# One scan for both directions: the backward state-space chunks fed in reverse, 159 columns instead of 190

## Chip, core and metric

The kernel runs on one core of one Trainium2 chip. The metric is the device time of one execution in microseconds (us). The engines are TensorE (PE; its weight loads are PEld), VectorE (DVE), ScalarE (ACT), GpSimd (POOL) and SyncE (SP), which issues most DMAs. They run in parallel, each in its own order of instructions, and wait for one another by semaphores.

## What is computed

One layer of a diffusion backbone: 1024 latent tokens and 256 context tokens of width 1024. A modulated RMS norm feeds one combined input projection, whose columns go to four head groups (convolution, Fourier mixing, neighbourhood attention, and a bidirectional state space); their outputs are normed, concatenated and projected, and a squared-ReLU MLP follows. The change lies in the state space, cut here to what matters:

```python
for dirn, reverse in ((0, False), (1, True)):
    lam = lax.complex(a_re[dirn], a_im[dirn])               # 16 groups x 64 states
    dt = jnp.exp(log_dt[dirn])[:, None]
    a_bar = jnp.exp(lam * dt)
    b_bar = ((a_bar - 1) / lam)[..., None] * lax.complex(b_re[dirn], b_im[dirn])
    c_mat = lax.complex(c_re[dirn], c_im[dirn])
    h_c = diag_scan(a_bar, jnp.einsum("blgm,gpm->blgp", ucc, b_bar), reverse)
    h0 = h_c[:, 0] if reverse else h_c[:, -1]                # the context's last state
    bu_x = jnp.einsum("blgm,gpm->blgp", uxc, b_bar)
    bu_x = bu_x.at[:, edge].add(a_bar * h0)
    h_x = diag_scan(a_bar, bu_x, reverse)
    y_x = y_x + jnp.einsum("blgp,gmp->blgm", h_x, c_mat).real
```

## The kernel before, in words

The order around the state space is not written by hand: a scheduler orders each engine's instructions by a modelled timeline, and tiles come from pools that are stacked in the on-chip memory; a tile that lies where an earlier one lay waits for that one's readers. So a change of size in one pool can move instructions far from it.

The first 130 us hold the modulation (`gv_rows`, L151), the norm of the latent tokens (`nt`, `xl`), the first projection tiles, and the context's norm and products (L210, L242 to L244). A projection tile is 24 matmuls of 128x512 (L364), three for each of eight chunks, on weights that ScalarE and GpSimd split into a high and a low part (`whi`, `wlo`, L231 to L235).

The state space works on chunks of eight tokens: 16 channels by 8 tokens make the 128 rows of `U` (columns: 32 chunks of context, 128 of latent tokens, and the 32 of context again). Partitions 0 to 63 hold the forward states, 64 to 127 the backward ones.

- *Small setup* (pools `ssm` and `tiny`, L434 to L581): from `log_dt` by exponential, sine and powers (tiles `t_...`, `pw`, `pa`, `pb`) to the input weights `bb`, on GpSimd and VectorE in turn, most of it 16 columns wide.
- *`ssm_setup(b)`*, for each of eight batches of two groups: GpSimd and VectorE make `wn` (the chunk's input weights; TensorE transposes them by `pt` into `wt`) and `ca` (its output weights); ScalarE copies parts of `ca` into the zero-padded `cx_`; TensorE makes the chunk's inner kernel `pk` from it, which goes through DRAM into the Toeplitz tile `tz`.
- *`ssm_tables(b)`*: sine and cosine of the phase of each chunk index (`nidx`), on VectorE and ScalarE.
- *`ssm_main(b)`*: the chunk products `ps` (L682) over NQ = 190 columns; a rotation by the tables (`ro`, L687 to L692, VectorE and GpSimd); the scans with the real decay (L697 forward, L698 backward with its operands read in reverse), 64 partitions each; the rotation back (`hr`, L701 to L706); and the output products `py`, three for each group (L710 `tz` by `U`, L711 and L712 `ca` by `hr`).

Setup and tables of batch b+1 are written ahead of main b. Beside all that TensorE runs projection tiles. The convolution's input `cv` (L782) comes after them, on VectorE, when its tile is done.

Of the kernel before, what the change touches and what calls it, by code (L numbers as in the profile page):

```python
# [8 lines left out]
F32 = mybir.dt.float32  # L9
# [3 lines left out]
ALU = mybir.AluOpType  # L13
# [4 lines left out]
P = 128  # L18
# [4 lines left out]
MAGIC = 12582912.0  # L23
TWO_PI = 6.2831845
PI_ = 3.14159225
NQ = 190

COLS = {}
_n = 0
# [20 lines left out]
def body(tc, A, out, dbg=None):  # L50
    nc = tc.nc
    V, S, G, PE, SP = nc.vector, nc.scalar, nc.gpsimd, nc.tensor, nc.sync
# [349 lines left out]
    for hf in range(2):  # L402
        for ti in FIRST:
            o = x_tile(cw[ti], hf, (("mm", "gn"), ("at", "gv"))[hf][ti == 8])
# [14 lines left out]
    for m in range(2):  # L419
        o = c_tile(cw[12 + m])  # L420
# [15 lines left out]
    sp = open_pool("ssm", "right", stack=sset)  # L436
# [141 lines left out]
    bm = sp.tile([P, 2, 16, 32], F32, name="bm")  # L578
# [4 lines left out]
    GB = 2  # L583
# [9 lines left out]
    def tms(name, w):  # L593
        return sp.tile([P, GB, w], F32, name=name, tag="ss", bufs=4)

    cx_ = sp.tile([P, 2, GB, 240], F32, name="cx_")
    G.memset(cx_, 0.0)

    def ssm_setup(b):
        g0 = GB * b  # L600
        gs = slice(g0, g0 + GB)

        pbx = lambda t: t[:, :, gs].rearrange("p j g -> p g j")[:, :, :, None].to_broadcast([P, GB, 8, 16])
        bbx = lambda t: t[:, gs, None, :].to_broadcast([P, GB, 8, 16])
        wn = [tms(f"wn{i}", P) for i in range(2)]
        t1, t2 = tms("ws1", P), tms("ws2", P)
        G.tensor_tensor(v4(wn[0]), pbx(pb_r), bbx(bb_r), ALU.mult)
        G.tensor_tensor(v4(t1), pbx(pb_i), bbx(bb_i), ALU.mult)
        V.tensor_tensor(wn[0], wn[0], t1, ALU.subtract)
        G.tensor_tensor(v4(wn[1]), pbx(pb_r), bbx(bb_i), ALU.mult)  # L610
        G.tensor_tensor(v4(t2), pbx(pb_i), bbx(bb_r), ALU.mult)
        V.tensor_tensor(wn[1], wn[1], t2, ALU.add)

        ca = sp.tile([P, 2, GB, 160], F32, name="ca", tag="ca", bufs=3)
        pax = lambda t: t[:, :, gs].rearrange("p s g -> p g s")[:, :, :, None].to_broadcast([P, GB, 10, 16])
        cx = lambda i: b3(cn[:, i, :])[:, gs, None, :].to_broadcast([P, GB, 10, 16])
        t1, t2 = tms("cs1", 160), tms("cs2", 160)
        G.tensor_tensor(v4(ca[:, 0]), pax(pa_r), cx(0), ALU.mult)
        G.tensor_tensor(v4(t1), pax(pa_i), cx(1), ALU.mult)
        G.tensor_tensor(ca[:, 0], ca[:, 0], t1, ALU.subtract)  # L620
        G.tensor_tensor(v4(ca[:, 1]), pax(pa_r), cx(1), ALU.mult)
        G.tensor_tensor(v4(t2), pax(pa_i), cx(0), ALU.mult)
        V.scalar_tensor_tensor(ca[:, 1], ca[:, 1], -1.0, t2, ALU.mult, ALU.subtract)

        pk = st_tile("pk")
        fw, bw = slice(0, 64), slice(64, 128)
        S.copy(cx_[fw, :, :, 112:240], ca[fw, :, :, 0:128])
        S.copy(cx_[bw, :, :, 0:128], ca[bw, :, :, 32:160])
        for g in range(GB):
            for i in range(2):  # L630
                PE.matmul(pk[32 * g:32 * g + 32, 0:240], bm[:, i, g0 + g, :], cx_[:, i, g, :],
                          start=i == 0, stop=i == 1, skip_group_check=True)
        kt_ = sp.tile([32 * GB, 240], F32, name="kt_", tag="kt_", bufs=2)
        S.copy(kt_, pk[:32 * GB, :240])
        V.scalar_tensor_tensor(kt_[:, 112:128], K("idk")[:32 * GB], C("ssm_d", b)[:32 * GB],
                               kt_[:, 112:128], ALU.mult, ALU.add)
        tz = sp.tile([P, GB, P], F32, name="tz", tag="tz", bufs=3)
        for g in range(GB):
            o_ = (g0 + g) * 240
            SP.dma_start(ap(kb, o_, [[3840, 16], [1, 240]]), kt_[32 * g:32 * g + 16, :])  # L640
            SP.dma_start(tz[:, g, :], ap(kb, o_, [[16, 8], [3840, 16], [1, 128]]))
        wt = sp.tile([P, GB, 2, P], F32, name="wt", tag="wt", bufs=3)
        pt = st_tile("pt")
        for g in range(GB):
            for i in range(2):
                PE.transpose(pt[:, (2 * g + i) * P:(2 * g + i + 1) * P], wn[i][:, g, :], ident)
        S.copy(wt.rearrange("p a b c -> p (a b c)"), pt[:, :2 * GB * P])
        return ca, tz, wt

    def ssm_tables(b):  # L650

# [16 lines left out]
        V.tensor_scalar(fl(cst_), fl(cst_), -2.0, 1.0, ALU.mult, ALU.add)  # L668
        return snt, cst_

    def ssm_main(b, ca, tz, wt, snt, cst_):
        g0 = GB * b
        U = sp2.tile([P, GB, 192], F32, name="U", tag="U", bufs=2)
        for g in range(GB):
# [2 lines left out]
        Ss = sp2.tile([P, 2, GB, NQ], F32, name="Ss", tag="Ss", bufs=2)  # L677
        for g in range(GB):
            ps = at_tile("ps")
            for i in range(2):  # L680
                for d in range(2):
                    PE.matmul(ps[64 * d:64 * d + 64, i * NQ:(i + 1) * NQ], wt[:, g, i, 64 * d:64 * d + 64],  # L682
                              U[:, g, 2 * d:2 * d + NQ], start=True, stop=True, skip_group_check=True)
            S.copy(Ss[:, :, g, :], ps[:, :2 * NQ].rearrange("p (i q) -> p i q", i=2))
        s_r, s_i = fl(Ss[:, 0]), fl(Ss[:, 1])
        r1, r2, r3, r4 = [tmp(f"ro{i}", NQ, t) for i, t in enumerate(("ra", "rc", "rb", "rc"))]
# [5 lines left out]
        V.tensor_tensor(fl(r3), fl(r3), fl(r4), ALU.subtract)  # L692
        for i, src in ((0, r1), (1, r3)):
            for g in range(GB):
                f_, b_ = slice(0, 64), slice(64, 128)
                r_ = rho[:, g0 + g:g0 + g + 1].to_broadcast([P, NQ])
                V.tensor_tensor_scan(Ss[f_, i, g, :], r_[f_], src[f_, g, :], 0.0, ALU.mult, ALU.add)  # L697
                V.tensor_tensor_scan(Ss[b_, i, g, ::-1], r_[b_], src[b_, g, ::-1], 0.0, ALU.mult, ALU.add)  # L698
        xs = slice(31, 159)
        h1, h2_, h3, h4 = [tmp(f"hr{i}", P, t) for i, t in enumerate(("ra", "rc", "rb", "rc"))]  # L700
        V.tensor_tensor(h1, Ss[:, 0, :, xs], cst_[:, :, xs], ALU.mult)  # L701
# [6 lines left out]
        for g in range(GB):  # L708
            o = py[:, g * P:(g + 1) * P]
            PE.matmul(o, tz[:, g, :], U[:, g, 32:160], start=True, stop=False)  # L710
            PE.matmul(o, ca[:, 0, g, 16:144], h1[:, g, :], start=False, stop=False)  # L711
            PE.matmul(o, ca[:, 1, g, 16:144], h3[:, g, :], start=False, stop=True)  # L712
        yt = tmp("yt", P, "yt")
        S.copy(fl(yt), py[:, :GB * P])
        for g in range(GB):
# [26 lines left out]
    for tb in range(10):  # L742
        o = mm_tile()
        pairs = []
        for k in range(8):
            if tb < 8:
                hf, b = divmod(tb, 4)
                a_, b_ = hh[hf][k][:, b * P:(b + 1) * P], hl[hf][k][:, b * P:(b + 1) * P]
            else:
                b = tb - 8  # L750
                a_, b_ = ch[k][:, b * P:(b + 1) * P], cl[k][:, b * P:(b + 1) * P]
# [91 lines left out]
    for m in range(2):  # L843
        t = q4("eo")
# [22 lines left out]
    for m in range(2):  # L867
# [25 lines left out]
    for m in range(2):  # L893
# [6 lines left out]
        f = q4("ff")  # L900
# [13 lines left out]
    for hf in range(2):  # L914
        sl = slice(hf * H, (hf + 1) * H)
        yf = q4("yf").rearrange("p (m c) -> p m c", m=2)
        for m in range(2):
            ms = slice(m * P, (m + 1) * P)
            o = (at_tile, st_tile)[m]("fo")
# [509 lines left out]
    for k in range(3, 8):  # L1429
# [3 lines left out]
        o = mm_tile()  # L1433
# [444 lines left out]
def shape_constants():  # L1878
# [6 lines left out]
        bd[0, s, s] = np.cos(ang) / 256  # L1885
        bd[1, s, s] = np.sin(ang) / 256
    nidx = np.zeros((P, NQ))
    nidx[:64] = np.arange(NQ)
    nidx[64:] = NQ - 1 - np.arange(NQ)
    sel = np.zeros((P, 2))  # L1890
    for q in range(4):
        for v in range(2):
# [42 lines left out]
```

## Time and profile before

| | us |
|---|---|
| median of 3 runs (1337.73 to 1339.29) | 1338.77 |
| the profiled execution, its own time | 1341.13 |
| its span in the trace | 1339.0 |
| TensorE busy in the span | 1197.4 (89%) |
| VectorE busy | 1068.4 (80%) |
| GpSimd busy | 808.6 (60%) |
| ScalarE busy | 652.7 (49%) |

The profiled execution took 2.13 us more than its span, and 2.36 more than the median. Shares over the whole span mix stages with different limits, so the state space is read by stretches: it lies between 127.7 us (the first `ps`) and 270 us (the last `py`), and the convolution begins at 282.7.

### The profile page before, as it was taken

The numbers are of one execution on the slowest core, as the hardware profiler recorded it, in microseconds if no ns is written. First come the engines' busy times: TensorE is split into PE (matmuls) and PEld (weight loads), VectorE is DVE, ScalarE is ACT, GpSimd is POOL, SyncE is SP. The second block draws the span as 40 slices with busy tenths as digits, with TensorE's granted clock in tenths as the row PEclk, the third lists the DMA queues.
The fourth block names the chain that finished last, engine by engine and source line by source line (L and its number), as shares of the span: only waits on it lengthen the run. The fifth ranks groups of instructions, "written<-read, shape, count | busy, mean of one in ns | idle before, by whom it ended". The sixth has DMA issues, their size and how long they took to land.

```text
span 1339.0 us, 18718 instructions
## 1 busy us (share of the span) xinstructions
PE 1197.4 (89%) x6188; PEld 965.5 (72%) x6188; DVE 1068.4 (80%) x1636; ACT 652.7 (49%) x1337; POOL 808.6 (60%) x1002
## 2 busy tenths in 40 slices
PE   5889878898865999899999999999999999999996
PEld 3657656777655777777778777777877777777775
DVE  4775999869999768658695579888888888888867
ACT  5254333323446565554664445555545555444555
POOL 3825677372556734015367477777877778787754
PEclk9989898998975999898999999999999999999998
DMA  9455232161153544323121121111211112211113
GB/s 344 142 164 164 81 125 79 47 199 66 51 177 94 175 128 142 109 78 143 32 77 43 40 64 32 48 56 56 63 56 32 52 52 63 64 41 39 56 40 126
DMA packets 75058, 121.77 MB, mean 91 GB/s; under 512 B 16977, under 2 KB 35154, under 8 KB 74962
## 3 DMA queue, kind: packets, MB, share of 16 engines
q1 hardware_dynamic: 62802, 113.24, 26.9%
q10 hardware_dynamic: 12160, 7.34, 1.8%
q8 instruction: 49, 0.80, 0.3%
q14 instruction: 47, 0.39, 0.1%
HBM read 106.68 MB, written 13.88 MB: 90 GB/s over the span
## 4 chain that ended last, share of the span: by engine, by line
PE 48%; DVE 29%; ACT 5%; issue 4%; POOL 4%; DMA 3%; SPq 1%; ACTq 0%; DVEq 0%; POOLq 0%
PE fa L1472 11%; PE qa L1472 6%; PE qb L1472 5%; PE fb L1472 5%; DVE cacc L1015 5%; DVE tl L1488 3%; PE fc L1472 2%; DVE fl L1488 2%; PE f L1472 2%; PE p_t L1270 2%; PE mm L1097 2%; PE mm L1472 2%; DVE Ss L698 2%; DVE Ss L697 1%; DVE X L1493 1%
## 5 line engine op out<-in xcount | busy, mean ns | idle before, releaser
L1456 POOL TENSOR_TENSOR w2l<-w2r,w2h 128x128 fp32r<-128x128 f32 (+1 forms) x232 | 177.4, 766 | 75.3 <-ACT w2h L1455 68.1
L1493 DVE SCALAR_TENSOR_TENSOR X<-fa,gt2c,X 128x512 f32<-128x512 f32 x216 | 159.4, 745 | 13.0 <-PE fa L1472 13.0
L1455 ACT ACTIVATE w2h<-w2r 128x128 fp32r<-128x128 f32 (+1 forms) x232 | 85.8, 387 | 150.8 <-POOL w2r L1706 79.8
L1456 POOL TENSOR_TENSOR w2l<-w1r,w2h 128x256 fp32r<-128x256 f32 x136 | 108.5, 814 | 57.7 <-ACT w2h L1455 34.0
L235 POOL TENSOR_TENSOR wlo<-wraw,whi 128x1024 fp32r<-128x1024 f32 x30 | 75.2, 2508 | 102.0 <-ACT whi L233 82.9
L1493 DVE SCALAR_TENSOR_TENSOR X<-fb,gt2c,X 128x512 f32<-128x512 f32 x108 | 80.5, 745 | 35.4 <-PE fb L1472 35.3
L1456 POOL TENSOR_TENSOR w2l<-ws,w2h 128x256 fp32r<-128x256 f32 x84 | 67.9, 815 | 41.4 <-ACT w2h L1455 40.1
L1015 DVE SCALAR_TENSOR_TENSOR cacc<-cv,wdw,cacc 128x512 f32<-128x512 f32 x92 | 92.3, 1047 | 0.6
L364 PE MATMUL mm<-xl,whi 128*128 128x512 f32 x192 | 81.2, 424 | 3.8 <-DVE xl L220 3.8
L364 PE MATMUL mm<-xh,whi 128*128 128x512 f32 x192 | 77.3, 423 | 7.0 <-ACT xh L218 5.8
L1472 PE MATMUL fa<-th,w2h 128*128 128x512 f32 x156 | 63.2, 405 | 19.7 <-DVE X L1493 19.7
L364 PE MATMUL mm<-xh,wlo 128*128 128x512 f32 x192 | 80.6, 420 | 0.0
L1455 ACT ACTIVATE w2h<-w1r 128x256 fp32r<-128x256 f32 x136 | 53.9, 409 | 47.5 <-DVE w1r L1609 16.5
L1472 PE MATMUL qa<-cb,w2h 128*128 128x512 f32 x224 | 70.7, 397 | 0.7 <-ACT ft L1624 0.7
L1488 DVE TENSOR_TENSOR fl<-ft,fh 128x512 fp32r<-128x512 f32 x64 | 56.9, 906 | 12.8 <-ACT fh L1487 12.7
L1472 PE MATMUL fa<-th,w2l 128*128 128x512 f32 x156 | 61.7, 396 | 0.6 <-POOL w2l L1456 0.6
L1472 PE MATMUL fa<-tl,w2h 128*128 128x512 f32 x156 | 61.5, 394 | 0.0
L1013 POOL TENSOR_TENSOR pacc<-pacc,ptmp 128x512 f32<-128x512 f32 x24 | 37.4, 1559 | 29.8 <-ACT ptmp L1012 29.8
L1455 ACT ACTIVATE w2h<-ws 128x256 fp32r<-128x256 f32 x84 | 33.1, 410 | 42.4 <-DVE ws L1605 20.4
L1472 PEld LDWEIGHTS fa<-th,w2h 128*128 128x128 f32 x156 | 29.3, 188 | 30.8 <-DVE X L1493 25.2
L364 PEld LDWEIGHTS mm<-xh,whi 128*128 128x128 f32 x192 | 38.1, 201 | 18.4 <-ACT xh L218 7.2
L1472 PEld LDWEIGHTS qa<-cb,w2h 128*128 128x128 f32 x224 | 42.0, 188 | 11.2 <-ACT ft L1624 1.1
(788 smaller groups left out, 3945.3 us busy)
## 6 DMA issues: line engine op xcount, KB each, us to landing
w2r<-in_w_ff SPq DMA_DIRECT2D x68, 256.0 KB
wmB<-in_wmodB SPq DMA_DIRECT2D x32, 512.0 KB
w1r<-in_w_ff SPq DMA_DIRECT2D x64, 256.0 KB
wm<-in_wmodA SPq DMA_DIRECT2D x16, 512.0 KB
wraw<-in_w_in SPq DMA_DIRECT2D x12, 512.0 KB
x<-in_xT SPq DMA_DIRECT2D x8, 512.0 KB
wraw<-in_w_out SPq DMA_DIRECT2D x8, 512.0 KB
kr<-k_d SPq DMA_DIRECT2D x16, 256.0 KB
```

Source lines behind the costliest of these rows:

```text
L235: (lo_eng or G).tensor_tensor(lo, raw, hi.bitcast(F32), ALU.subtract)
L364: PE.matmul(o, a_[:, k, :], b_[hf][k], start=k == 0 and i == 0, stop=k == 7 and i == 2)
L698: V.tensor_tensor_scan(Ss[b_, i, g, ::-1], r_[b_], src[b_, g, ::-1], 0.0, ALU.mult, ALU.add)
L1013: G.tensor_tensor(pacc, pacc, t, ALU.add)
L1015: V.scalar_tensor_tensor(acc, x(k), w(k), acc, ALU.mult, ALU.add)
L1097: PE.matmul(o, a_[:, 2 * kk + c, :], b_, start=c == 0 and i == 0, stop=c == 1 and i == 2)
L1270: PE.matmul(po[:, j * 64:j * 64 + 64], ptt[:, i * P:(i + 1) * P], rv, start=i == 0, stop=i == 4, skip_group_check=True)
L1455: S.activation(hi, a, AF.Copy)
L1456: G.tensor_tensor(lo, a, hi.bitcast(F32), ALU.subtract)
L1472: PE.matmul(o, a_[:, i, :], m_, start=start and j == 0, stop=stop and j == 2, skip_group_check=True)
L1488: V.tensor_tensor(lo, t, hi.bitcast(F32), ALU.subtract)
L1493: return V.scalar_tensor_tensor(x, o, gt2(k), x, ALU.mult, ALU.add).ins
```

## The change

NQ goes from 190 to 159. The backward half of `ps` reads `U` in reverse, from its last column down, so that both directions run in the same sense: one scan does all 128 partitions (L701 after), 32 scans for 64, and all tables and rotations are 159 columns wide. The chunk index `nidx` counts upward on all partitions. Since the backward states now stand in reverse, one product can't take both directions to the output: `h1` and `h3` have each one product with the forward weights and one with the backward weights that reads `hr` in reverse (L716, L717 after), which makes five for three in each group. These weights are taken from the zero-padded tile, which grows from 240 to 272 columns and has three buffers (`cx0` to `cx2`), each held until its batch's output; `ca` has one buffer instead of three.

```diff
-NQ = 190
+NQ = 159
...
-    cx_ = sp.tile([P, 2, GB, 240], F32, name="cx_")
-    G.memset(cx_, 0.0)
+
+
+    cxs = [sp.tile([P, 2, GB, 272], F32, name=f"cx{i}") for i in range(3)]
+    for t in cxs:
+        G.memset(t, 0.0)
...
-        ca = sp.tile([P, 2, GB, 160], F32, name="ca", tag="ca", bufs=3)
+        ca = sp.tile([P, 2, GB, 160], F32, name="ca", tag="ca", bufs=1)
+        cx_ = cxs[b % 3]
...
-        S.copy(cx_[fw, :, :, 112:240], ca[fw, :, :, 0:128])
-        S.copy(cx_[bw, :, :, 0:128], ca[bw, :, :, 32:160])
+        S.copy(cx_[fw, :, :, 128:272], ca[fw, :, :, 0:144])
+        S.copy(cx_[bw, :, :, 0:144], ca[bw, :, :, 16:160])
...
-                PE.matmul(pk[32 * g:32 * g + 32, 0:240], bm[:, i, g0 + g, :], cx_[:, i, g, :],
+                PE.matmul(pk[32 * g:32 * g + 32, 0:240], bm[:, i, g0 + g, :], cx_[:, i, g, 16:256],
...
-                              U[:, g, 2 * d:2 * d + NQ], start=True, stop=True, skip_group_check=True)
+                              U[:, g, 191:191 - NQ:-1] if d else U[:, g, 0:NQ], start=True, stop=True,
+                              skip_group_check=True)
...
-                f_, b_ = slice(0, 64), slice(64, 128)
                 r_ = rho[:, g0 + g:g0 + g + 1].to_broadcast([P, NQ])
-                V.tensor_tensor_scan(Ss[f_, i, g, :], r_[f_], src[f_, g, :], 0.0, ALU.mult, ALU.add)
-                V.tensor_tensor_scan(Ss[b_, i, g, ::-1], r_[b_], src[b_, g, ::-1], 0.0, ALU.mult, ALU.add)
+                V.tensor_tensor_scan(Ss[:, i, g, :], r_, src[:, g, :], 0.0, ALU.mult, ALU.add)
...
-            PE.matmul(o, ca[:, 0, g, 16:144], h1[:, g, :], start=False, stop=False)
-            PE.matmul(o, ca[:, 1, g, 16:144], h3[:, g, :], start=False, stop=True)
+
+            for i, h in enumerate((h1, h3)):
+                PE.matmul(o, cx_[:, i, g, 144:272], h[:, g, :], start=False, stop=False)
+                PE.matmul(o, cx_[:, i, g, 0:128], h[:, g, ::-1], start=False, stop=i == 1)
...
-    nidx[:64] = np.arange(NQ)
-    nidx[64:] = NQ - 1 - np.arange(NQ)
+    nidx[:] = np.arange(NQ)
```

The pool `ssm` grows by 4096 bytes a partition: `cx_` and three buffers of `ca` were 11,520 bytes, three `cx` and one `ca` are 15,616. The pool `tiny` above it slides by as much, and its first tiles come to lie where the modulation's `gv_rows` lies. The engines' orders differ in many places, of which three matter here.

On VectorE, the chain of small tiles (`t_dr`, L454, is its first step that needs `log_dt`) stood among the modulation's and the norm's operations. Before:

```order
L215 SCALAR_TENSOR_TENSOR nt<-x,gsc,acc 128x512
L210 TENSOR_TENSOR acc<-acc,sq 128x512 x2
L220 SCALAR_TENSOR_TENSOR xl<-nt,mod,xh 128x512
L210 TENSOR_TENSOR acc<-acc,sq 128x512 x5
L454 SCALAR_TENSOR_TENSOR t_dr<-t_dn,t_ldt 128x16
L455 SCALAR_TENSOR_TENSOR t_dr<-t_dn,t_dr 128x16
L458 SCALAR_TENSOR_TENSOR t_dw<-t_dw,t_dr 128x16
```

After, at the end of the modulation:

```order
L215 SCALAR_TENSOR_TENSOR nt<-x,gsc,acc 128x512 x2
L220 SCALAR_TENSOR_TENSOR xl<-nt,mod,xh 128x512 x2
L497 MEMSET pw_r 128x16
L498 MEMSET pw_i 128x16
L509 RECIPROCAL t_iv<-t_iv 128x16
L210 TENSOR_TENSOR acc<-acc,sq 128x256 x7
L454 SCALAR_TENSOR_TENSOR t_dr<-t_dn,t_ldt 128x16
L455 SCALAR_TENSOR_TENSOR t_dr<-t_dn,t_dr 128x16
L458 SCALAR_TENSOR_TENSOR t_dw<-t_dw,t_dr 128x16
```

The chain moved behind the last `xl` and behind the context's sum of squares, the seven `acc` of 128x256; all of the setup follows it.

On GpSimd, the place of the first rotation `ro`, in the main part of batch 0. The numbers in the names tell the batches' tiles apart: `wn_1438` and `cs_1449` are batch 3's, and those of the row `cs_1336` are batch 2's. Before:

```order
L676 COPY U<-U 128x2x32
L608 TENSOR_TENSOR ws_1440<-pb_i,bb_i 128x256
L676 COPY U<-U 128x2x32
L610 TENSOR_TENSOR wn_1439<-pb_r,bb_i 128x256
L688 TENSOR_TENSOR ro_1287<-Ss,snt 128x380
L690 TENSOR_TENSOR ro_1289<-Ss,snt 128x380
L611 TENSOR_TENSOR ws_1441<-pb_i,bb_r 128x256
L619 TENSOR_TENSOR cs_1449<-pa_i,cn 128x320
L622 TENSOR_TENSOR cs_1450<-pa_i,cn 128x320
L702 TENSOR_TENSOR hr_1305<-Ss,snt 128x256
L704 TENSOR_TENSOR hr_1307<-Ss,snt 128x256
L688 TENSOR_TENSOR ro_1400<-Ss,snt 128x380
```

After (line numbers are three to five higher), first the rows from batch 0's last `ca` on, through batch 1's setup (`wn_1216`, `cs_1227`):

```order
L624 TENSOR_TENSOR ca<-ca,cs_1170 128x320
L610 TENSOR_TENSOR wn_1216<-pb_r,bb_r 128x256
L611 TENSOR_TENSOR ws_1218<-pb_i,bb_i 128x256
L622 TENSOR_TENSOR ca<-pa_r,cn 128x320
L613 TENSOR_TENSOR wn_1217<-pb_r,bb_i 128x256
L625 TENSOR_TENSOR ca<-pa_r,cn 128x320
L614 TENSOR_TENSOR ws_1219<-pb_i,bb_r 128x256
L623 TENSOR_TENSOR cs_1227<-pa_i,cn 128x320
L626 TENSOR_TENSOR cs_1228<-pa_i,cn 128x320
L624 TENSOR_TENSOR ca<-ca,cs_1227 128x320
```

and directly behind them, with batch 2's setup (`wn_1329`, `cs_1340`):

```order
L610 TENSOR_TENSOR wn_1329<-pb_r,bb_r 128x256
L611 TENSOR_TENSOR ws_1331<-pb_i,bb_i 128x256
L622 TENSOR_TENSOR ca<-pa_r,cn 128x320
L625 TENSOR_TENSOR ca<-pa_r,cn 128x320
L613 TENSOR_TENSOR wn_1330<-pb_r,bb_i 128x256
L693 TENSOR_TENSOR ro_1291<-Ss,snt 128x318
L695 TENSOR_TENSOR ro_1293<-Ss,snt 128x318
L614 TENSOR_TENSOR ws_1332<-pb_i,bb_r 128x256
L623 TENSOR_TENSOR cs_1340<-pa_i,cn 128x320
L705 TENSOR_TENSOR hr_1305<-Ss,snt 128x256
L707 TENSOR_TENSOR hr_1307<-Ss,snt 128x256
L626 TENSOR_TENSOR cs_1341<-pa_i,cn 128x320
```

Before, three batches' setup was done and a fourth begun when the first `ro` came. After, one batch's setup precedes these rows, fourteen setup products of the next two stand between it and the first `ro`, and there are two setup products, for three, between the pair of `ro` and the pair of `hr`.

On TensorE, the place of the first `ps`, batch 0's, before:

```order
L364 MATMUL mm<-xh,wlo 128x512
L364 MATMUL mm<-xh,whi 128x512
L682 MATMUL ps<-U,wt 64x190 x8
L631 MATMUL pk<-cx__1153,bm 32x240 x4
L646 MATMUL pt<-ident,wn_1325 128x128
L646 MATMUL pt<-ident,wn_1326 128x128
L646 MATMUL pt<-ident,wn_1325 128x128
L646 MATMUL pt<-ident,wn_1326 128x128
L364 MATMUL mm<-xl,whi 128x512
```

And the place of the first `pk` and `pt`, batch 0's too, after:

```order
L364 MATMUL mm<-xh,wlo 128x512
L635 MATMUL pk<-cx_1153,bm 32x240 x4
L650 MATMUL pt<-ident,wn_1159 128x128
L650 MATMUL pt<-ident,wn_1160 128x128
L650 MATMUL pt<-ident,wn_1159 128x128
L650 MATMUL pt<-ident,wn_1160 128x128
L364 MATMUL mm<-xh,whi 128x512
L364 MATMUL mm<-xl,whi 128x512
L364 MATMUL mm<-xh,wlo 128x512
L242 MATMUL mm<-ch,whi 128x256
```

Before, the `pk` and `pt` of two batches had come long before the first `ps`, and 175 projection matmuls of 128x512 and 72 context products stood ahead of it. After, the first `pk` comes 20 context products and three wide ones ahead of the first `ps`, which has 192 and 92 ahead of it. At the other end, 47 matmuls of projection tiles that the convolution needs stand ahead of the last batch's `py` on `hr`, and 24 before.

## Rows read from the trace of the kernel before

**Rows 1.** Stretches of the one core; the header names the columns.

```profile
core 0: us, PE busy (x) PEld busy (x) DVE busy (x) ACT busy (x) POOL busy (x), PEclk, DMA share, GB/s
0.00:28.00 28.00, 13.35 (x71) 9.06 (x75) 13.82 (x38) 15.77 (x27) 6.24 (x15) 1.00 0.96 353
...
54.00:82.00 28.00, 23.93 (x136) 17.52 (x135) 26.20 (x45) 10.00 (x18) 18.44 (x24) 0.94 0.39 131
...
127.70:282.70 155.00, 131.03 (x852) 103.69 (x852) 133.48 (x192) 50.92 (x106) 97.17 (x93) 0.91 0.31 95
129.70:270.10 140.40, 116.55 (x775) 92.00 (x769) 131.04 (x185) 47.12 (x101) 89.29 (x86) 0.90 0.26 79
272.50:282.70 10.20, 10.20 (x46) 8.19 (x45) 0.03 (x2) 2.49 (x3) 5.59 (x7) 1.00 0.73 243
282.70:420.00 137.30, 108.74 (x482) 89.51 (x480) 134.38 (x169) 58.34 (x89) 70.08 (x44) 0.85 0.37 116
```

**Rows 2.** TensorE's timeline: start, us, line, operation, operands, count [idle before].

```profile
127.69 1.51 PE L682 MATMUL ps<-U,wt 128*64 128x190 f32 x16
...
132.19 0.38 PE L710 MATMUL py<-U,tz 128*128 128x128 f32 x2
132.33 0.48 PE L364 MATMUL mm<-xh,wlo 128*128 128x512 f32 x1
...
141.68 0.49 PE L711 MATMUL py<-hr,ca 128*128 128x128 f32 x2 [2.18 <-DVE hr L705]
...
270.22 0.49 PE L712 MATMUL py<-hr,ca 128*128 128x128 f32 x2 [1.11 <-DVE hr L706]
```

**Rows 3.** List of waits, 128 to 280 us: total us, times, longest.

```profile
POOL hr L702 <- DVE Ss L698: 34.5, 8, 5.9
...
PE py L711 <- DVE hr L705: 11.7, 5, 3.9
```

**Rows 4.** VectorE's timeline: the chain of small tiles, and L782.

```profile
25.90 0.18 DVE L454 SCALAR_TENSOR_TENSOR t_dr<-t_dn,t_ldt 128x16 f32<-128x16 f32 x1 [0.83 <-POOL t_dn L453]
...
45.13 0.16 DVE L502 SCALAR_TENSOR_TENSOR t_mr<-t_cm,t_Em 128x16 f32<-128x16 f32 x1
...
90.97 0.43 DVE L210 TENSOR_TENSOR acc<-acc,sq 128x256 f32<-128x256 f32 x1 [0.90 <-ACT sq L209]
...
282.69 0.69 DVE L782 SCALAR_TENSOR_TENSOR cv<-cth,mm 128x512 f32<-128x512 f32 x1 [10.17 <-PE mm L364]
```

**Rows 5.** VectorE's groups, 128 to 280 us: busy us, mean ns, idle before.

```profile
L698 DVE TENSOR_TENSOR_SCAN Ss<-t_rho,ro 64x190 f32<-64x190 f32 x32 | 21.2, 664 | 0.4
L697 DVE TENSOR_TENSOR_SCAN Ss<-t_rho,ro 64x190 f32<-64x190 f32 x32 | 20.0, 625 | 0.3
```

**Rows 6.** VectorE's timeline: plain operations and scans of two batches.

```profile
132.88 0.54 DVE L692 TENSOR_TENSOR ro<-ro,ro 128x380 f32<-128x380 f32 x1
133.35 0.99 DVE L697 TENSOR_TENSOR_SCAN Ss<-t_rho,ro 64x190 f32<-64x190 f32 x1
...
135.32 0.55 DVE L697 TENSOR_TENSOR_SCAN Ss<-t_rho,ro 64x190 f32<-64x190 f32 x1
135.88 0.55 DVE L698 TENSOR_TENSOR_SCAN Ss<-t_rho,ro 64x190 f32<-64x190 f32 x1
...
158.09 0.41 DVE L706 TENSOR_TENSOR hr<-hr,hr 128x256 f32<-128x256 f32 x1
```

**Rows 7.** ScalarE's timeline: one of the copies into `cx_`.

```profile
76.63 0.62 ACT L628 COPY cx__1153<-ca 64x512 f32<-64x512 f32 x1
```

**Rows 8.** GpSimd's timeline: a setup product, a weight split, the first `ro`.

```profile
57.20 0.63 POOL L607 TENSOR_TENSOR wn<-pb_r,bb_r 128x256 f32<-128x256 f32 x1
...
114.29 2.38 POOL L235 TENSOR_TENSOR wlo<-wraw,whi 128x1024 fp32r<-128x1024 f32 x1 [1.51 <-ACT whi L233]
...
129.80 1.38 POOL L688 TENSOR_TENSOR ro<-Ss,snt 128x380 f32<-128x380 f32 x1 [2.42 <-ACT Ss L684]
```

**Rows 9.** GpSimd's timeline: the `cs` product that runs beside two scans.

```profile
133.89 1.00 POOL L619 TENSOR_TENSOR cs<-pa_i,cn 128x320 f32<-128x320 f32 x1
```

More of the change, by code (lines that the diff above doesn't have):

```diff
@@ L647, in ssm_setup @@
         S.copy(wt.rearrange("p a b c -> p (a b c)"), pt[:, :2 * GB * P])
-        return ca, tz, wt
+        return cx_, tz, wt
     def ssm_tables(b):
@@ L669, in ssm_tables, with ssm_main @@
         return snt, cst_
-    def ssm_main(b, ca, tz, wt, snt, cst_):
+    def ssm_main(b, cx_, tz, wt, snt, cst_):
         g0 = GB * b
```

## Prediction

> **What bounds the kernel now.** First the table of stretches [rows 1]. From 127.7 to 282.7 us the state space runs beside the input projection: TensorE works 131.03 of 155.00 us, and in its core, 129.7 to 270.1, VectorE works 131.04 of 140.40. Neither is a wall by itself. Then the rows of TensorE [rows 2]: the first output product on `hr` (L711) starts at 141.68 and the last batch's (its L712) at 270.22. That is seven batch steps, 128.5 us, 18.4 each. The list of waits [rows 3] says who holds whom inside a step: TensorE waits 11.7 us for VectorE's `hr`, and GpSimd waits 34.5 us, once in each of the eight batches, for the second half of the scans. So the scans stand on a batch's chain, and VectorE is what TensorE waits for. After the last batch TensorE never rests (10.20 of 10.20 us, 272.5 to 282.7, 46 products of 0.22 us), and VectorE is idle for 10.17 us until the convolution's first input (L782) at 282.69 [rows 1, 4]. From there to 420 VectorE works 134.38 of 137.30: what is won or lost by 282.69 is carried on, I assume to the end. The quantity to forecast is when L782 starts.
>
> **Scans.** 64 scans of 64x190 took 21.2 + 20.0 = 41.2 us, mean 0.64 [rows 5]; an undisturbed one takes 0.55 in either direction [rows 6]. 32 remain, on all partitions, over 159 columns. Plain operations give the fixed part: 380 columns 0.54, 256 columns 0.41, so 1.05 ns a column and 0.14 us fixed; a scan is then (0.55 - 0.14)/190 = 2.1 ns a column, and 159 columns take 0.48 (bounds 0.46, in proportion, and 0.55, unchanged). With the 0.09 that disturbance added before (0.64 - 0.55), four scans of 0.57 replace 5.15 us in each batch: 2.3, a gain of 2.85 (bounds 2.4 and 3.3).
>
> **Other columns.** Some ten VectorE operations a batch go from 380 to 318 columns: 10 x 62 x 1.05 ns = 0.65, some of them dearer and some cheaper per column; I take 0.5. GpSimd's two `ro` products shrink too, and have slack.
>
> **Output products.** The order shows five matmuls for three in each of 16 groups. One is 132.33 - 132.19 = 0.14 us [rows 2], so 4 x 0.14 = 0.56 a batch. Eight `ps` products a batch were 1.51/8 = 0.19 and become about 0.16: -0.24. Reading the operand reversed is not in the trace. Its bounds are nothing and a doubling of the eight reversed products a batch, 4 x 0.16 + 4 x 0.14 = 1.2 us (8.4 over seven steps). VectorE's reversed scan costs what the forward one does (0.55 both), the nearest row there is; I take nothing.
>
> **Smaller terms.** Two more memsets of `cx` come in GpSimd's first microseconds, when it works 6.24 of 28 us [rows 1]: nothing. The ScalarE copies, 0.62 us [rows 7], widen by 144/128 to 0.70; ScalarE works 50.92 of 155 [rows 1]. Three `cx` buffers free `pk`'s input; in exchange `ca` has one buffer, so GpSimd's first `ca` product of a batch waits for the copies of the batch before, and behind it on GpSimd stand the `ro` and `hr` of an earlier batch, for which VectorE waits. With half a batch of lead between them I price that at 2 us, once, at the start (bounds 0 and 1 us a batch).
>
> **What moves.** The larger `cx` pushes the small setup tiles onto memory that the modulation's `gv_rows` still holds, and the order shows the result: the chain that begins with `t_dr` stood among the modulation's work, and now stands behind the context's last sum of squares. In the trace `t_dr` is at 25.90, `t_mr` at 45.13, that sum ends at 91.40 [rows 4]. Without the modulation's wide operations between, I take 12 us for the 19.2 from `t_dr` to `t_mr` (bounds 7 and 19.2): 103.4. From `t_mr` to GpSimd's first `wn` was 57.20 - 45.13 = 12.1 [rows 4, 8], and two `ca` products now stand ahead of it: 117. Then in order four products of 0.8, two weight splits of 2.4, two copies of `U`, two `cs` and a `ca` of about 1 [rows 8]: 11.7, so 128.7; VectorE's `ca` and the copies, 1.8: the first `pk` may start at 130.5. Next GpSimd has fourteen setup products of batches 1 and 2 ahead of the first `ro`: 14 x 0.9 (they run between 0.63 and 1.00 [rows 8, 9]) + 2 = 14.6 from 128.7 on, hence `ro` at 143.3, where it was 129.80 [rows 8]: +13.5. The first 82 us lose VectorE's small operations, with which it was busy 26.20 of 28 in the last 28 [rows 1]; I give that 2 us. So the start comes 11.5 us later (bounds 5 and 19), and the first output product, less 2.5 for that batch's scans, at 150.7. What covers the delay is the context's and the projection's products done ahead meanwhile: TensorE does 17 wide ones before the first `ps` that stood behind it.
>
> **The sum.** VectorE per step: 131.04 x 18.4/140.4 = 17.2, less 2.85 and 0.5: 13.85. TensorE per step: 116.55 x 18.4/140.4 = 15.3, plus 0.56, less 0.24: 15.6. TensorE takes VectorE's place, and I take 16.0 a step, 0.4 above it. Bounds: 18.4, all waits kept; and 14.5, VectorE's 13.85 and a little, if the clock granted to TensorE, 0.90 in this stretch, rises as its waits go. Seven steps: 150.7 + 112 = 262.7. From there to L782 were 282.69 - 270.22 = 12.5 us; the order has 47 projection products ahead of the last output group for 24 before, 23 x 0.22 = 5.1 fewer behind: 7.4. L782 at 270.1, 12.6 us earlier. The profiled execution took 1341.13: 1328.5. It stood 2.36 above the median of the runs: **1326**.
>
> **Rivals.**
> (a) *Slower: the setup is late and the chain stays serial.* GpSimd's `ro` waits behind setup with the one `ca` buffer, each batch keeps its 18.4 and the start is 18 late: 160 + 128.8 + 7.4 = 296.2, +13.5, 1352. For it: only 11.7 of TensorE's 24 us of idle time are put down to `hr`, and VectorE's gain is nothing if GpSimd comes last. Against: GpSimd works 89.29 of 140.40 and 34.5 of its idle time ends with the scans. It decides from a step of 17.8 us on.
> (b) *No change: the late start eats the gain.* Steps of 17.7: 150.7 + 123.9 + 7.4 = 282, 1338.
> (c) *GpSimd collides more.* A scan takes 0.99 beside GpSimd's `cs` of 133.89, 0.55 without it [rows 6, 9]. GpSimd now waits less for scans, and works more beside them: 32 x 0.43 = 13.8 us at most, 1.7 a batch instead of the 0.36 counted: steps of 17.2, 278.5, 1334.5.
> The Trainium skill, "SBUF — State Buffer", "Who interferes with whom", says that a VectorE instruction with two inputs in SBUF and a GpSimd instruction that reads SBUF exclude each other, and the later one stands still. The 0.99 beside the 0.55 agrees; by that rule alone the stretch would go as (c) does.
> (d) *More.* The start 5 late and steps of 14.5: 147 + 101.5 + 7.4 = 255.9, 1312.
> (e) *Reversed reads cost TensorE double*: +8.4, 1334.5.
>
> **Chances.** Forecast with its own spread (1318 to 1333) 0.50, (a) 0.18, (b) 0.12, (c) 0.08, (e) 0.04, (d) 0.08. The range reaches to 1312 below, where (d) is, and to 1346 above, into (a), leaving most of (a)'s upper half out. A measurement of this kernel can tell 0.2%, 2.7 us, from no change: faster means below 1336.1. Faster: 0.50 + 0.08 + most of (c) and (e), 0.68. Same: (b) mostly, 0.12. Slower: (a) and a little of (b), 0.20.
>
> **What would show it.** The scans at 0.46 to 0.55, 32 of them, some 18 us together (mean 0.57) confirm their term; 0.9 and more is (c). The first `ro` of GpSimd at 140 to 145 confirms the late setup, and at 130 refutes it. Steps between the output products near 16, with TensorE seldom idle, confirm the sum; 18 with waits on ScalarE's `cx` or GpSimd's `ro` is (a). `ps` reads of 0.3 us instead of 0.16 are (e). L782 near 270 and an unchanged distance from there to the end close the account. The prediction is wrong first if setup is not late at all (then about 1315), or if GpSimd, not VectorE, sets the step.

## The result

The changed kernel took 1321.09 us (median of 4 runs, 1319.62 to 1321.68) against 1338.47 us: 0.9877 of the time before, 95% interval [0.9853, 0.9901], 17.4 us faster by the medians. The prediction was 1326 us, 12.8 faster than the median it was made against, in a range of 1312 to 1346. The profiled execution took 1320.52 us, with a span of 1318.4, 20.6 shorter than the span before; the medians, not the two profiles, are the result.

What answers to [rows 1], the table of stretches (same columns):

```profile
54.00:82.00 28.00, 26.10 (x190) 19.97 (x182) 15.31 (x46) 11.19 (x25) 1.65 (x8) 0.93 0.49 146
127.70:282.70 155.00, 142.76 (x962) 115.71 (x961) 124.94 (x182) 56.58 (x116) 108.71 (x113) 0.97 0.35 109
129.70:270.10 140.40, 129.15 (x892) 104.92 (x891) 111.39 (x171) 52.06 (x110) 95.75 (x104) 0.96 0.32 99
140.90:254.70 113.80, 102.71 (x743) 84.36 (x744) 95.17 (x148) 43.65 (x95) 79.07 (x86) 0.96 0.32 98
```

In the same 140.40 us VectorE works 111.39 us instead of 131.04, TensorE 129.15 instead of 116.55, at a granted clock of 0.96 for 0.90; the last 7 us of this stretch belong to the convolution now. The last row is the seven steps, from batch 0's first product on `hr` to the last batch's.

TensorE's timeline, for [rows 2]:

```profile
128.01 1.30 PE L686 MATMUL ps<-U,wt 128*64 128x159 f32 x16
...
140.93 0.49 PE L716 MATMUL py<-hr,cx 128*128 128x128 f32 x2 [0.19 <-DVE hr L708]
141.26 0.39 PE L717 MATMUL py<-hr,cx 128*128 128x128 f32 x2
...
254.69 0.38 PE L716 MATMUL py<-hr,cx 128*128 128x128 f32 x2
254.91 0.39 PE L717 MATMUL py<-hr,cx 128*128 128x128 f32 x2
255.13 0.39 PE L716 MATMUL py<-hr,cx 128*128 128x128 f32 x2
```

The first product on `hr` is where it was (141.68 before). The steps are (254.69 - 140.93)/7 = 16.25 us. Before, counted by the same product, the last batch's L711, they were (268.48 - 141.68)/7 = 18.1; the 18.4 of the prediction ended at L712.

```profile
268.48 0.38 PE L711 MATMUL py<-hr,ca 128*128 128x128 f32 x2
```

The rows of the changed kernel that stand 0.22 us apart also show that L717, which reads `hr` in reverse, takes as long as L716, which reads it forward.

The list of waits from 90 to 280 us, for [rows 3] (engine, line and what it waited for: total us, times, longest):

```profile
POOL hr L705 <- DVE Ss L701: 12.8, 7, 2.5
...
POOL ca L622 <- ACT cx L632: 4.9, 4, 3.3
```

and TensorE's, from 138 to 262 us:

```profile
PE py L716 <- DVE hr L708: 2.2, 2, 2.0
PE py L713 <- ACT yt L719: 1.5, 1, 1.5
```

GpSimd's wait for the scans is down from 34.5 us to 12.8, and TensorE's for `hr`, 11.7 and 2.7 before, is 2.2. New is GpSimd's wait for ScalarE's copies out of the one `ca` buffer.

VectorE's timeline, for [rows 4], and its scans from 128 to 280 us, for [rows 5]:

```profile
78.86 0.42 DVE L210 TENSOR_TENSOR acc<-acc,sq 128x256 f32<-128x256 f32 x1 [0.52 <-ACT sq L209]
79.21 0.17 DVE L454 SCALAR_TENSOR_TENSOR t_dr<-t_dn,t_ldt 128x16 f32<-128x16 f32 x1
...
90.28 0.18 DVE L502 SCALAR_TENSOR_TENSOR t_mr<-t_cm,t_Em 128x16 f32<-128x16 f32 x1
...
262.81 0.69 DVE L787 SCALAR_TENSOR_TENSOR cv<-cth,mm 128x512 f32<-128x512 f32 x1 [5.74 <-PE mm L364]
```

```profile
L701 DVE TENSOR_TENSOR_SCAN Ss<-t_rho,ro 128x159 f32<-128x159 f32 x32 | 16.9, 580 | 0.0
```

The scans took 16.9 us for 41.2, mean 0.58 us for one. The convolution's first input (L787 now) came at 262.81 for 282.69. GpSimd's timeline, for [rows 8]:

```profile
103.56 0.71 POOL L610 TENSOR_TENSOR wn<-pb_r,bb_r 128x256 f32<-128x256 f32 x1
...
114.18 0.95 POOL L624 TENSOR_TENSOR ca<-ca,cs 128x320 f32<-128x320 f32 x1
...
132.84 0.75 POOL L693 TENSOR_TENSOR ro<-Ss,snt 128x318 f32<-128x318 f32 x1
```

The first `ro` came at 132.84 us for 129.80: 3 us later, not the 13.5 that were forecast.

Last, the chain that ended last inside the state space, by line, first before (128 to 282 us), then after (128 to 262):

```profile
by line: issue 13.9%; DVE Ss L698 13.9%; DVE Ss L697 11.9%; DVE ph L659 4.9%; DVE ro L692 3.4%; POOL wlo L235 3.3%; SPq L972 3.1%; DVE ph L657 2.8%; PE ps L682 2.8%; DMA wraw<-in_w_in 2.6%; DVE ro L691 2.2%; DVE hr L706 2.2%; DVE ro L687 1.
```

```profile
by line: PE mm L364 8.5%; issue 7.0%; PE mm L244 5.8%; DVE Ss L701 5.8%; PE mm L242 5.4%; PE mm L243 5.3%; DVE ca L627 4.4%; PE py L716 4.1%; PE py L717 3.8%; PE ps L686 3.7%; DVE ph L663 3.5%; DVE ph L666 3.4%; ACTq L721 3.1%; DVE ro L697 
```

Scans held 25.8% of the chain and hold 5.8%; of the lines that are named first now, TensorE has most.

### The profile page after: what moved, and what is told of

The parts are those of the page before. It is cut to its first block, busy times and chain, and to the rows that moved or that the text cites. A ratio compares the mean times of both kernels' runs of the same rounds, so it can differ in the third digit from the quotient of the medians.

```text
span 1318.4 us, 18813 instructions
## 1 busy us (share of the span) xinstructions
PE 1182.3 (90%) x6252; PEld 961.2 (73%) x6252; DVE 1025.8 (78%) x1604; ACT 650.7 (49%) x1335; POOL 799.6 (61%) x1004
## 4 chain that ended last, share of the span: by engine, by line
PE 52%; DVE 27%; ACT 5%; POOL 3%; DMA 3%; issue 3%; SPq 1%; ACTq 0%; DVEq 0%; POOLq 0%
PE fa L1477 11%; PE qa L1477 6%; PE qb L1477 6%; PE fb L1477 5%; DVE cacc L1020 3%; DVE tl L1493 3%; PE fc L1477 2%; PE p_t L1275 2%; PE mm L1102 2%; DVE fl L1493 2%; PE mm L364 2%; PE mm L1477 2%; DVE X L1498 1%; PE p_t L1263 1%; PE f L1477 1%
## 5 line engine op out<-in xcount | busy, mean ns | idle before, releaser
L1020 DVE SCALAR_TENSOR_TENSOR cacc<-cv,wdw,cacc 128x512 f32<-128x512 f32 x92 | 85.1, 971 | 0.4
L364 PE MATMUL mm<-xh,wlo 128*128 128x512 f32 x192 | 77.8, 407 | 0.0
L1018 POOL TENSOR_TENSOR pacc<-pacc,ptmp 128x512 f32<-128x512 f32 x24 | 41.0, 1708 | 25.4 <-ACT ptmp L1017 25.4
L1484 ACT ACTIVATE ft<-ft,colf 128x512 f32<-128x512 f32 x42 | 30.5, 727 | 35.4 <-DVE ft L1632 35.4
```

Of the source, the lines that this page charges most:

```text
L364: PE.matmul(o, a_[:, k, :], b_[hf][k], start=k == 0 and i == 0, stop=k == 7 and i == 2)
L1018: G.tensor_tensor(pacc, pacc, t, ALU.add)
L1020: V.scalar_tensor_tensor(acc, x(k), w(k), acc, ALU.mult, ALU.add)
L1484: S.activation(t, t if src is None else src, AF.Relu, bias=CF("b_ff1", f))
```

## The experiments

Each is compared with the kernel before on the same chip by the ratio of times, with a 95% interval. The kernels ran in three sets (e1 to e4; e5, e6, e8 and after_again; e7, e9, e10 and e2_again), each on one chip; there the single runs of the kernel before spread over 5 to 10 us and those of the others over 4 to 19, so differences of 3 us between two kernels are not told apart. A profiled execution is one of these runs: that of e8 is its slowest (1351.88 us, median 1341.11), that of e9 its fastest (1315.19, median 1321.51). In this table *first* and *last* are the starts of the first product on `hr` in batch 0 and in the last batch, and *step* is a seventh of the distance, in the profiled execution.

| kernel | what it is | ratio to before | first, last (us) | step |
|---|---|---|---|---|
| before | | 1 | 141.68, 268.48 | 18.1 |
| changed | | 0.9877 [0.9853, 0.9901] | 140.93, 254.69 | 16.3 |
| after_again | changed, beside e5, e6, e8 | 0.9887 [0.9867, 0.9908] | 140.08, 253.76 | 16.2 |
| e1_move_only | before, small tiles moved | 1.0098 [1.0062, 1.0134] | 144.33, 286.81 | 20.4 |
| e2_all_but_move | changed, tiles not moved | 0.9869 [0.9839, 0.9899] | 137.26, 241.27 | 14.9 |
| e3_two_scans | changed, scans cut in two | 1.0064 [1.0041, 1.0087] | 142.23, 275.05 | 19.0 |
| e8_split_no_move | e2, scans cut in two | 1.0009 [0.9985, 1.0033] | 140.84, 265.87 | 17.9 |
| e4_forward_reads | changed, no reversed reads | 0.9874 [0.9836, 0.9911] | 145.07, 259.19 | 16.3 |
| e5_three_products | changed, 32 products fewer | 0.9891 [0.9870, 0.9912] | 140.22, 255.71 | 16.5 |
| e6_short_scans | changed, scans of 16 columns | 0.9865 [0.9838, 0.9892] | 138.34, 244.70 | 15.2 |
| e9_merged_190 | merged scans over 190 columns | 0.9835 [0.9819, 0.9851] | 135.41, 247.11 | 16.0 |
| e10_no_move_kt1 | changed, tiles not moved | 0.9881 [0.9864, 0.9897] | 141.11, 245.23 | 14.9 |
| e7_ca_two | e2 with two `ca` buffers | 0.9854 [0.9824, 0.9884] | 141.21, 244.87 | 14.8 |
| e2_again | e2, beside e7, e9, e10 | 0.9859 [0.9825, 0.9893] | 142.99, 248.12 | 15.0 |

**The move alone.**

```diff
+    pad = tp.tile([P, 1024], F32, name="pad")
+    G.memset(pad[:, 0:1], 0.0)
     E_ = G
     ldt = tn("ldt")
```

> The kernel before with an unused tile of 4096 bytes a partition at the head of the pool of small tiles, and no other edit: the small chain moves behind the context's sum of squares as it does in the changed kernel, the scans and widths stay. Theory (the late setup is paid for by a modulation that runs undisturbed, so the move is worth about nothing): the context's last sum of squares ends near 79 us, the first output product on hr stands at 141 to 145 us, and the time is 1335 to 1342 us. First rival (the move is itself most of the gain, because the front is 12 us shorter): 1325 to 1330. Second rival (the prediction's term, the late start of 9 us, holds when the scans are long): 1346 to 1350.

It lost 1%, some 13 us (9.4 by the medians), so the move is not worth nothing where the scans are long. Its rows:

```profile
78.32 0.43 DVE L210 TENSOR_TENSOR acc<-acc,sq 128x256 f32<-128x256 f32 x1 [0.52 <-ACT sq L209]
...
144.33 0.49 PE L713 MATMUL py<-hr,ca 128*128 128x128 f32 x2 [0.69 <-DVE hr L707]
...
286.81 0.38 PE L713 MATMUL py<-hr,ca 128*128 128x128 f32 x2
```

```profile
POOL hr L704 <- DVE Ss L700: 32.0, 8, 5.4
...
PE py L713 <- DVE hr L707: 21.5, 6, 6.7
```

The context's last sum of squares ends at 78.75 us, as in the changed kernel and 12.7 earlier than before (91.40), and the first product on `hr` is only 2.7 late. So the late setup does not cost at the start. It costs in the steps, 20.4 us for 18.1: TensorE's wait for `hr` is 21.5 us for 11.7, and GpSimd, which now has more of the setup there, works 95.06 us between the first and the last product on `hr` (144.60 us), for 82.31 before (129.31 us). The time fits the second rival, but not its reason. The convolution's first input is where it was before (282.69), though the span is 6.4 us longer, so in this kernel it does not tell when the end comes:

```profile
282.77 0.69 DVE L784 SCALAR_TENSOR_TENSOR cv<-cth,mm 128x512 f32<-128x512 f32 x1
```

**All but the move.**

```diff
-    cxs = [sp.tile([P, 2, GB, 272], F32, name=f"cx{i}") for i in range(3)]
+    cxs = [(sp2 if i == 2 else sp).tile([P, 2, GB, 272], F32, name=f"cx{i}") for i in range(3)]
```

> The changed kernel with the third cx buffer in the later pool of the main part, so that the small tiles don't slide and their chain stays among the modulation's work as before. Theory (the move is worth nothing, the gain is in the steps): steps of about 16.3 us, 1318 to 1324 us. First rival (the move is most of the gain): 1328 to 1333. Second rival (the move costs 9 us): 1309 to 1314.

The same gain as the changed kernel. The steps were shorter than expected, 14.9 us, and the state space ends earlier (last batch at 241 for 255 us), but more projection products are left behind it, and the convolution's first input came at 267.05, later than 262.81:

```profile
267.05 0.68 DVE L787 SCALAR_TENSOR_TENSOR cv<-cth,mm 128x512 f32<-128x512 f32 x1
```

**Scans cut in two, with the move and without it.**

```diff
-                V.tensor_tensor_scan(Ss[:, i, g, :], r_, src[:, g, :], 0.0, ALU.mult, ALU.add)
+                for h_ in (slice(0, 64), slice(64, 128)):
+                    V.tensor_tensor_scan(Ss[h_, i, g, :], r_[h_], src[h_, g, :], 0.0, ALU.mult, ALU.add)
```

> The changed kernel with each scan over 128 partitions cut in two scans over 64, both forward: 64 scans of 64x159, everything else as changed. They add 32 x 0.57 = 18 us to VectorE. Theory (scans stand on each batch's chain, though VectorE has some room in the changed kernel, 12.9 us of work in a step of 16.3): half of it shows, 1327 to 1333 us, and GpSimd's wait for the scans grows from 12.8 us to some 25. Rival (TensorE is the bound now, and VectorE has room): under 1324. Rival (VectorE is the bound): 1336 or more.

This is the second rival's case, VectorE as the bound: 1.0064 for 0.9887 is 24 us above the changed kernel, more than the 34.3 - 16.9 = 17.4 us by which VectorE's scans grew:

```profile
L702 DVE TENSOR_TENSOR_SCAN Ss<-t_rho,ro 64x159 f32<-64x159 f32 x64 | 34.3, 537 | 0.8
```

```profile
by line: issue 18.3%; DVE Ss L702 15.7%; DVE ro L697 3.8%; DMA wraw<-in_w_in 3.5%; DVE ph L663 3.4%; DVE ph L666 3.1%; PE py L717 3.0%; PE mm L364 2.7%; ACTq L722 2.4%; DVE ro L696 2.3%; DVE wn L612 2.3%; PE py L718 2.1%; DVE hr L707 2.1%; 
```

The scans are again the costliest operation of the chain, and GpSimd's wait for them, expected at some 25 us, is 29.5 from 128 to 282 us. In the profiled executions the convolution's first input comes 16.0 us later than in the changed kernel:

```profile
278.80 0.69 DVE L788 SCALAR_TENSOR_TENSOR cv<-cth,mm 128x512 f32<-128x512 f32 x1 [0.85 <-PE mm L364]
```

What the time lost beyond that lies behind this point, and is not shown to be due to the scans. The same cut in e2, without the move:

> The kernel e2 (all of the change but the move) with each scan cut in two of 64 partitions. Theory (the move costs about 13 us where VectorE is the bound and nothing where it isn't, so what e3 lost to the kernel before was the move): 0.996 to 1.002 of the kernel before. Rival (cutting the scans costs 25 us, with the move or without it): 1.004 to 1.009 of it.

It is 1.0009, the kernel before to within its interval. The theory holds: with scans of 64 partitions the move costs (1.0009 to 1.0064 here, 1 to 1.0098 in e1); with scans of 128 it costs nothing that can be measured (0.9877 and 0.9887 with it, 0.9869, 0.9859 and 0.9881 without). And what the change has beside the merging and the move (narrower tables and scans, five output products, new buffers) is together worth nothing that can be measured.

**Reversed reads.**

```diff
-                              U[:, g, 191:191 - NQ:-1] if d else U[:, g, 0:NQ], start=True, stop=True,
+                              U[:, g, 0:NQ], start=True, stop=True,
...
-                PE.matmul(o, cx_[:, i, g, 0:128], h[:, g, ::-1], start=False, stop=i == 1)
+                PE.matmul(o, cx_[:, i, g, 0:128], h[:, g, :], start=False, stop=i == 1)
```

> The changed kernel with U and hr read forward by TensorE in the backward half; the backward direction's result is therefore not computed, the work is the same in size. Theory (a reversed read costs TensorE nothing): the same time as the changed kernel within 2 us, ps and py products of the same length. Rival (reversed reads cost): 1313 us, with ps and py products shorter than in the changed kernel.

The same time, and products 0.22 us apart as in the changed kernel:

```profile
185.28 0.38 PE L716 MATMUL py<-hr,cx 128*128 128x128 f32 x2
185.50 0.39 PE L717 MATMUL py<-hr,cx 128*128 128x128 f32 x2
185.72 0.39 PE L716 MATMUL py<-hr,cx 128*128 128x128 f32 x2
```

**What sets the step now.** Two kernels took work away, from TensorE and from VectorE:

```diff
-                PE.matmul(o, cx_[:, i, g, 144:272], h[:, g, :], start=False, stop=False)
-                PE.matmul(o, cx_[:, i, g, 0:128], h[:, g, ::-1], start=False, stop=i == 1)
+                PE.matmul(o, cx_[:, i, g, 144:272], h[:, g, :], start=False, stop=i == 1)
```

> The changed kernel without the second product of each pair (L717), so three output products a group as before; the backward direction's output is left out. That takes 32 products of 0.22 us, 7.0 us, from TensorE. Theory (with the scans merged, TensorE sets the step): 5 to 7 us faster than the changed kernel run beside it. Rival (the steps are still set by VectorE's and GpSimd's chain): within 2 us of it.

```diff
-                V.tensor_tensor_scan(Ss[:, i, g, :], r_, src[:, g, :], 0.0, ALU.mult, ALU.add)
+                V.tensor_tensor_scan(Ss[:, i, g, 0:16], r_[:, 0:16], src[:, g, 0:16], 0.0, ALU.mult, ALU.add)
```

> The changed kernel with each scan over 16 columns instead of 159; the scan of the other columns is left out. That takes some 11 us from VectorE, all of it in the batches' chains. Theory (TensorE sets the step): at most 3 us faster than the changed kernel. Rival (the scans are still on the chain that sets the time): 8 to 12 us faster.

The time of neither is told apart from the changed kernel beside them (0.9887). For e6 that was the theory's case; its scans took 8.8 us for 16.9:

```profile
L701 DVE TENSOR_TENSOR_SCAN Ss<-t_rho,ro 128x16 f32<-128x16 f32 x32 | 8.8, 326 | 0.0
```

But its steps did get shorter, 15.2 us for the 16.2 of after_again, by as much as a batch's scans lost, (16.9 - 8.8)/8 = 1.0. So the scans still stood in the steps. The last batch came 9.1 us earlier than in after_again, and yet the convolution's first input 3.4 us later than there (261.88), because TensorE still had projection products to do: it works 17.00 of the 17.00 us from 245 to 262. The two rows of e6:

```profile
244.70 0.38 PE L716 MATMUL py<-hr,cx 128*128 128x128 f32 x2
```

```profile
265.25 0.68 DVE L787 SCALAR_TENSOR_TENSOR cv<-cth,mm 128x512 f32<-128x512 f32 x1
```

For e5 the theory fell: 7 us of TensorE's work brought nothing in the step (16.5 us) nor in the time. With fewer products TensorE waited more, for `yt` copies of ScalarE and for `hr` (the changed kernel's rows are above):

```profile
PE py L713 <- ACT yt L718: 5.1, 2, 3.1
PE py L716 <- DVE hr L708: 4.3, 4, 2.2
```

So TensorE's products do not set the step of the changed kernel, and VectorE's scans do in part. In the table a step of 17.9 us or more goes with the time of the kernel before or a longer one; between 14.8 and 16.5 the time does not follow the step. What sets the time there was not isolated.

**Merged scans over 190 columns.** Here `kt_` has one buffer, which alone keeps the small tiles in their place; e10 is the same with 159 columns.

```diff
-NQ = 159
+NQ = 190
...
-        kt_ = sp.tile([32 * GB, 240], F32, name="kt_", tag="kt_", bufs=2)
+        kt_ = sp.tile([32 * GB, 240], F32, name="kt_", tag="kt_", bufs=1)
```

> The changed kernel over 190 columns again (NQ = 190), with the scans merged; kt_ has one buffer, which makes room for it and keeps the small tiles where they were, so there is no move. It adds to VectorE 32 x 0.07 us of scans and 62 columns in ten operations a batch, some 7 us in all, 2 us to TensorE and as much to GpSimd. Theory (the merging is the gain and VectorE has room once the scans are merged): 2 to 5 us slower than e10 beside it, 0.988 to 0.993 of the kernel before. Rival (the narrower tables are half of the gain): 8 us slower than e10 or more.

> The changed kernel with one buffer of kt_ instead of two, which alone keeps the small tiles off gv_rows, so that their chain stays among the modulation's work. Theory (the move is worth nothing in the changed kernel, as in e2): 0.985 to 0.990 of the kernel before, first ps at 113 us instead of 127. Rival (kt_ with one buffer delays pk): 0.992 or more.

e10's time is where it was expected (its first `ps` came at 117.0 us). e9 is not slower than it but faster, 0.9835 [0.9819, 0.9851] against 0.9881 [0.9864, 0.9897], the fastest kernel of the study, though its scans took longer:

```profile
L701 DVE TENSOR_TENSOR_SCAN Ss<-t_rho,ro 128x190 f32<-128x190 f32 x32 | 23.1, 774 | 0.0
```

So the narrower columns are no part of the gain, though they shorten the steps (14.9 us for 16.0). Why e9 is faster than e10 is not settled: the two differ in the scheduler's order all over the state space. In the profiled executions 4.3 us of the difference are there by the convolution's last input (340.0 and 344.3 us), and the rest comes between that and the MLP; but these are e9's fastest execution and one of e10's slowest.

**Two buffers of `ca`.**

```diff
-        ca = sp.tile([P, 2, GB, 160], F32, name="ca", tag="ca", bufs=1)
+        ca = sp.tile([P, 2, GB, 160], F32, name="ca", tag="ca", bufs=2)
```

> The kernel e2 (no move) with two buffers of ca instead of one. Theory (the single ca buffer costs some 2 us at most and not on the path): within 3 us of e2 beside it. Rival (GpSimd's waits for the copies of ca, 4.9 us in the changed kernel, are on the path): 4 us faster or more.

> The kernel e2 again, as the reference beside e7 and e10: 0.984 to 0.990 of the kernel before.

The two agree (0.9854 and 0.9859): the single buffer costs nothing that can be measured, as the theory had it.

## Why the prediction was right, and where it was off

The sign and the main term, the merged scans, held, and so did the length of the step, but not the reason given for it. The sum was 7 us short at the convolution's first input (270.1 forecast, 262.81 measured): the first product on `hr` came 9.8 us earlier than forecast, the steps took 1.8 us more and the tail 0.7.

- **Scans.** Forecast 2.85 us less a batch with 0.57 for one; measured (41.2 - 16.9)/8 = 3.04 with 0.58. The merged scan is as cheap as a half one. That the merging is the cause of the gain, e3 and e8 show: cut in two again, everything is lost.
- **Other columns.** With scans and columns VectorE was to work 13.85 us a step; it works 95.17/7 = 13.6. The size was right, but in the time it is worth nothing: e9 gives the columns back and loses nothing.
- **Output products.** Priced at 0.14 us from a distance of two rows, where the row that follows is of another kind; they stand 0.22 apart. Twice two groups of them are 0.88 us a batch, not 0.56. `ps` is 1.30/8 = 0.16, as forecast. The reversed read costs nothing, as taken (e4). The error did not matter, as e5 shows.
- **The step.** 16.0 forecast, 16.25 measured. The reason given for the number, that TensorE takes VectorE's place as the bound, is not shown, and the agreement is in part luck. TensorE works 102.71 of 113.80 us there and the chain is mostly its own, but e5 took work from it and the step stayed (16.5 us), while e6 took about as much from the scans and the step fell to 15.2.
- **The late start: the step that failed.** The move was seen and is there: `t_dr` stands behind the context's sum of squares, and from it on the pieces were nearly right: 11.1 us to `t_mr` (12 forecast), 13.3 from there to `wn` (13.6), 11.6 to the end of the last `ca` (11.7), 17.7 to the first `ro` (14.6; up to 3.3 of it a wait for the one `ca` buffer). But the sum of squares itself ended at 79.28 us instead of 91.40. For VectorE's small operations leaving the first 82 us the prediction gave 2 us; it was 12.1. By the prediction's own sign (the first `ro` at 140 to 145 confirms the late setup, at 130 refutes it) 132.84 is nearer to refuting it. The first product on `hr` came 9.8 us earlier than forecast (140.93 for 150.7), and this is more than all of the error. e1 shows it apart from the rest: with the move alone the front is as short. In every kernel with the move the sum of squares ends between 78 and 83 us, in every one without it between 87 and 92.
- **What hides the move.** In the changed kernel the front gains what the setup loses at the start. In the steps the move costs in either case: 16.3 us with it and 14.8 to 15.0 without it where the scans are merged, 20.4 for 18.1 and 19.0 for 17.9 where they are not. With merged scans the time does not show this: without the move the last batch comes earlier and the convolution's first input later (e2: 241.27 for 254.69, 267.05 for 262.81). With scans of 64 partitions the time shows it. There the move makes a slower kernel, as the forecast's rival (a) had it, but by its steps and not by a late start. Why it shows in the one case and not in the other was not isolated.
- **Rival (c), more collisions with GpSimd, did not come:** the scans lay 0.12 us above the shortest, 0.46, on average, 3.9 us in all; 9 of 32 ran beside a GpSimd operation. It came in kernels without the move (e10: 22.1 us of scans, mean 0.74, 14 of 32 beside GpSimd), and did not show in their time.
- **The tail and the end.** 7.4 us forecast from the last batch's product to L787, 262.81 - 254.69 = 8.1 measured. From there to the end of the span it was 1056.3 us before and is 1055.6, so the gain was carried, as assumed. But the assumption, that what is won or lost by L787 is carried to the end, does not hold in general, and that it fits here is in part luck. In the other kernels this distance lies between 1046.7 us (e2_again) and 1068.0 (e3); in e1 the first input came when it did before and the span was 6.4 us longer, in e2 it came 4.2 us later than in the changed kernel and the span was 3.3 us shorter. And in the second profile of the same changed kernel L787 was at 261.88 and the span 1324.7. These two differ between the convolution's last input and the MLP, where TensorE does the same 1935 matmul records in 389.70 and in 397.10 us, at a granted clock of 0.93 and of 0.91 (the changed kernel, then after_again); what makes the difference is not shown:

```profile
339.80:729.50 389.70, 335.51 (x1935) 281.39 (x1934) 292.85 (x501) 210.02 (x390) 184.39 (x148) 0.93 0.34 105
```

```profile
338.70:735.80 397.10, 338.99 (x1935) 284.81 (x1934) 294.43 (x501) 209.89 (x390) 181.14 (x148) 0.91 0.34 103
```

## What to carry to other kernels

A scan over half the partitions costs what one over all of them does (the shortest took 0.47 us for 64x159 in e3 and 0.46 for 128x159), so two directions belong in one instruction, even at the price of an operand read in reverse and of more products on another engine; the width of the scan mattered less than its count here. A small edit of a pool's size can move a chain of small operations across a stage: look at what the stage that they leave gains, not only at what the stage that they enter loses. And an engine's work is worth taking away where the chain of waits runs through it, and as long as that chain sets the time: cutting the merged scans in two again cost 19 us (e8 against e2) to 24 (e3 against the changed kernel), while taking 8 us more from them shortened the steps and brought nothing in the time that could be measured. A milestone that one pair of kernels shares, as the convolution's first input here, need not be what carries a gain to the end.

## What the runs showed of the hardware that was not expected

VectorE's operations in the modulation took much longer beside GpSimd's setup. A pair of `xl` of 128x512 took 2.41 us before, while GpSimd ran `cs` and `ca` products; in the changed kernel, with GpSimd idle, 1.41:

```profile
70.02 2.41 DVE L220 SCALAR_TENSOR_TENSOR xl<-nt,mod,xh 128x512 fp32r<-128x512 f32 x2
```

```profile
68.93 1.41 DVE L220 SCALAR_TENSOR_TENSOR xl<-nt,mod,xh 128x512 fp32r<-128x512 f32 x2
```

GpSimd worked 18.44 us between 54 and 82 us before and 1.65 after [rows 1], and VectorE's work there fell from 26.20 to 15.31 us; of these 10.9 us the setup operations that left VectorE are a part as well. The scans show the same one by one. Of the 64 scans before, the 52 during which GpSimd ran nothing took at most 0.55 us, and the 12 beside a GpSimd operation 1.07 on average; in e10 it was at most 0.48 us for 18, and 1.10 on average for 14. One scan that began inside a weight split of 2.59 us ended 0.42 us after it:

```profile
171.22 2.59 POOL L235 TENSOR_TENSOR wlo<-wraw,whi 128x1024 fp32r<-128x1024 f32 x1
```

```profile
171.68 2.55 DVE L698 TENSOR_TENSOR_SCAN Ss<-t_rho,ro 64x190 f32<-64x190 f32 x1
```

The Trainium skill, "SBUF — State Buffer", "Who interferes with whom", says that a VectorE instruction with two inputs in SBUF shuts out a GpSimd instruction that reads SBUF, and the other way round; these rows agree with it, though no kernel was run for it alone.

A matmul's moving operand read from its last column down costs the same as read forward (0.22 us either way, and e4 at 0.9874 for 0.9877 and 0.9887).
